# A two-layer hybrid decoder trunk: order and source of prefetched weight operands, and the place of side work

## The chip, the cores and the metric

The kernel runs on one core of one Trainium2 chip. The metric is device time in microseconds of one execution of the whole program; lower is better. The five engines appear below by the short names of the profile: PE (TensorE matmuls; PEld is its weight load), DVE (VectorE), ACT (ScalarE), POOL (GpSimd) and SP (SyncE, which here only issues DMAs).

## The reference

The input is one sequence of 1024 tokens of width 1024. Two layers follow one another. Each has a token mixer, a residual with layer norm, a squared-ReLU MLP of width 4096, a gated embedding and a second layer norm. The mixer of layer 0 is a causal pooling mixer, that of layer 1 a gated DeltaNet.

```python
for i in range(DEPTH):                       # DEPTH = 2
    mix = pool_mixer(...) if i % 2 == 0 else gated_deltanet(...)
    x = layer_norm(DEEPNORM_ALPHA * x + mix, ...)
    ff = square(relu(x @ mlp_w1[i])) @ mlp_w2[i]
    pe = sigmoid(x @ ple_gate_w[i] + ple_gate_b[i]) * (p[i] @ ple_proj[i])
    x = layer_norm(DEEPNORM_ALPHA * x + ff + pe, ...)

# gated_deltanet: 8 heads of 128, chunks of 64 tokens
proj = x @ w_in                              # Q, K, V, z (8 heads each) and two gate logits
q, k, v = silu(causal_conv(proj[Q, K, V], width=4)); q, k = l2norm(q), l2norm(k)
g = cumsum(-exp(a_log) * softplus(a_logit + dt_bias)); decay = exp(g_i - g_j), causal
m = eye + strict_lower(k_beta @ k.T * decay); u, w = triangular_solve(m, [v*beta, k_beta*exp(g)])
for chunk: v_new = u - w @ state
           o = (q*exp(g)) @ state + (q @ k.T * decay) @ v_new
           state = state * exp(g_last) + k_dec.T @ v_new
out = (rmsnorm(o) * norm_w * silu(z)) @ w_out
```

## The kernel before, in words

**Arithmetic.** Matrix products are made from float32 operands that are split in two parts: `split(hi, lo, src)` (L68, L69) copies on ACT to a rounded `hi` and subtracts on DVE to get `lo`. `mm3` (L73 to L75) then makes three matmuls of 128x512. The MLP, the gate's second half and most projections use a seven-product (Strassen-like) scheme over 2x2 blocks, whose products are named P1 to P7.

**Order of the instructions.** The text gives each step a place, and a scheduler then orders every engine's instructions with its own estimates of durations: a step that is ready while an engine is idle may stand some units ahead of its place in the text. Each engine and each DMA queue then runs strictly in that order, and waits where an operand or a free buffer is late. The buffers that matter are rotating slots: `tmp` (six of 128x512), `raw` (three of 128x1024), `wsm` with tags `wh` and `wl` (two each of 128x1024), `big` (ten of 128x4096) and eight PSUM banks.

**Stages, in order of time.** Layer 0's mixer and gate (0 to about 170 us); its MLP, `mlp(0, ...)`, with a phase A of 112 steps (`order`, up to about 487 us) and a phase B of 56 steps (`seq`, up to about 797 us); the projections of layer 1, `project(...)`, first in 18 units (`units`: the gate logits, K heads 0 to 7 and z heads 0 and 1, two halves of the sequence each), then in pairs of heads, `by_pairs` (957 to 1192 us); the chunk recurrence, `chain(...)` (`prepare` and `run`, eight chunks of 128 tokens, up to about 1345 us); the mixer's output product `mix_out` in two halves of the columns (to about 1440 us); layer 1's gate and `mlp(1, ...)` (1497 us to the end).

**Side work in the MLP of layer 0.** `mlp(0, ..., side=parts)` takes one of 101 closures at every second step of phase A (L544, while n is under 110) and, in phase B, two at each of the steps 24 to 39 and one at each step from 40 (L556). The first 13 closures (`k_parts`, L625) read the weights of K heads 2 to 7, split them and store both parts in DRAM (`wk_d`); the other 88 (`pair_parts`, L586) make the seven left operands of each of the 11 pairs and store them in `ws_d`.

**The units.** `weights(u + 1)` fetches the next head's operands before unit u's matmuls: `load_k` (L642) reads the two stored parts straight into `wh` and `wl`, `load_wsm` (L77) reads raw weights into a `raw` slot and splits them. After each unit's matmuls the side list of that unit runs: `gates` at unit 3 (DVE, ending in `g`, L842), `sums` at unit 5 (PE, L851), and pairs of `decay_rhs` (two POOL selects each, L862) at the units 5, 6, 8, 10, 11, 13, 15, 16, each followed one unit later by `decay` (two PE matmuls, an ACT exponential, a POOL select L874, a store to `dt_d`). `couple` makes the strictly lower matrices from them at the units 12 to 19 and stores them in `ad_d`, and `lanes_load` reads all of them back into `L` (2 MB, L926).

**The pairs.** In `by_pairs` the 77 products of 11 pairs run in the list `order`. `prep(n)` (L1000) loads the operand of product n from `ws_d` into one of seven slots, five products ahead. `head` runs the convolution on DVE (three instructions of 128x1023 to 128x1021, L1017) for Q and V heads, and two ACT instructions for z heads; `done` applies Silu and stores to `kqv_d`; `norm_q` transposes Q heads on PE (L1031). A forward substitution on `L` (`substitute(m)`, L942 and L944, m from 62 down to 1) is spread over the products up to number 67 by a running budget, from product 6 on. `load0` starts the loads of chunk 0 near the end.

**The chain.** `load_kqv(n)` loads K, Q and V of a chunk from POOL's DMA queue; `load(n)` loads the triangular blocks (`X`, `a_d`), `t11` from `t_d`, the gates `szt` on SP, and the decays `dt` (L1249, 512 KB into a `raw` slot) and `kt` on POOL's queue. `kq`, `kv`, `merge_a`, `merge_b`, `solve`, `state_in`, `state_out`, `output`, `norm` and `turn` are the steps of a chunk; `turn` scales the output on ACT (L1361), transposes it on PE (L1366) and multiplies by the gates (L1367). `embed1` runs beside it, with small loads `praw` on SP (L226). After the last chunk `fill` holds the products of `mix_out(..., nh=0)`; `mix_left` splits their left operand into `wsm` slots for even t and `raw` slots for odd t.

Of the kernel before, what the change touches and what calls it, by code (L numbers as in the profile page):

```python
# [7 lines left out]
F32 = mybir.dt.float32  # L8
# [24 lines left out]
def trunk(ctx: ExitStack, tc: tile.TileContext, io: dict):  # L33
# [286 lines left out]
    def mlp(i, r1, cut_t3, acc, row, finish=None, ahead=None, out=None, side=()):  # L320
# [21 lines left out]
        with tc.tile_pool(name=f"mlp{i}", bufs=5) as q:  # L342
# [192 lines left out]
            for n, o in enumerate(order):  # L535
                if n + 3 < len(order):
                    prep_a(*order[n + 3])
                if n == len(order) - 2:

                    for c in range(4):  # L540
                        load_w2(c)
                    prep_b(*seq[0])
                multiply_a(*o)
                if side and 2 <= n < 110 and n % 2 == 0:  # L544
                    side.pop(0)()
            for n, (k, g) in enumerate(seq):
# [9 lines left out]
                for _ in range(2 if 24 <= n < 40 else n >= 40):  # L556
                    if side:
                        side.pop(0)()
# [24 lines left out]
    pairs = [("Q", 0), ("V", 0), ("z", 2), ("Q", 2), ("V", 2), ("z", 4), ("Q", 4), ("V", 4), ("Q", 6), ("V", 6), ("z", 6)]  # L583
# [39 lines left out]
    wk_d = [dram.tile([P, 2, 2, 512], F32, name=f"wk{h}_d", tag=f"wk{h}_d") for h in range(2, 8)]  # L623

    def k_parts(h, z):  # L625

        t = {}

        def load():
            t["w"] = new_tmp(F32, "w")  # L630
            nc.sync.dma_start(t["w"], io["w_in"][jof["K"] + h][:, 4 * z:4 * z + 4, :].rearrange("p k c -> p (k c)"))

        def cut():
            hi, lo = new_tmp(F32R, "hi"), new_tmp(F32R, "lo")
            split(hi, lo, t.pop("w"))
            for a, r in enumerate((hi, lo)):
                nc.sync.dma_start(wk_d[h - 2][:, a, z], r.bitcast(F32))

        return load, cut

    def load_k(h):
        w = [wsm.tile([P, 8, P], F32R, tag=t, name=nm(t)) for t in ("wh", "wl")]  # L642
        for a, t in enumerate(w):
            nc.sync.dma_start(t.bitcast(F32).rearrange("p k c -> p (k c)"), wk_d[h - 2][:, a].rearrange("p z c -> p (z c)"))
        return w

    def staggered(pairs):

        pairs = list(pairs)
        return [pairs[0][0]] + [lambda a=a, b=b: (a[1](), b[0]()) for a, b in zip(pairs, pairs[1:])] + [pairs[-1][1]]  # L650

    parts = staggered(k_parts(h, z) for h in range(2, 8) for z in range(2))
    parts += [f for p in range(len(pairs)) for f in pair_parts(p)]
# [140 lines left out]
    def project(gd, pool, x2, left, first, g, ex, ahead, load0):  # L794
# [191 lines left out]
        def by_pairs(pool, ts, b):  # L986
# [13 lines left out]
            def prep(n):  # L1000
                p, k = order[n]
                tag, pl_ = slots[n % 7]
                o = pl_.tile([P, 2, 4, P], F32R, tag=tag, name=nm("wp"))
                nc.sync.dma_start(o.bitcast(F32).rearrange("p z k c -> p (z k c)"), ws_d[p][k].rearrange("p z c -> p (z c)"))
                st.setdefault(p, dict(op={}, ps={}))["op"][k] = o
# [72 lines left out]
            for n, (p, k) in enumerate(order[:last]):  # L1078
                room += 2.72 - (0.4 if pairs[p][0] == "z" else 1.45)
                while n > 5 and m > 0 and (room > 0 or n == last - 1):  # L1080
                    steps.setdefault(n, []).append(m)
                    room -= 0.4 + 2.1e-3 * m * (63 - m)
                    m -= 1
# [35 lines left out]
        at(5, sums)  # L1119
        todo = [(gi, n) for gi in range(2) for n in range(8)]  # L1120
        for k, (gi, n) in enumerate(todo):
            u = (5, 6, 8, 10, 11, 13, 15, 16)[k // 2]
# [56 lines left out]
        def weights(k):  # L1179
            if k < len(units):  # L1180
                s, h, hf = units[k]
                key = (s, h)
                if key not in w:
                    w[key] = load_k(h) if s == "K" else load_wsm(io["w_in"][jof[s] + h])
# [30 lines left out]
    def chain(gd, g, ex):  # L1215
# [19 lines left out]
        def load(n):  # L1235
# [13 lines left out]
            G.dma_start(dt, dt_d[n].rearrange("g p c -> p g c"))  # L1249
# [106 lines left out]
        def turn(n, gi):  # L1356
            d = pre[n]
            o = d["c"][:, 6 + gi]
            for j in range(4):
                c = 16 + gi * 4 + j  # L1360
                A.activation(o[:, j], o[:, j], AF.Copy, scale=d["f"][:, c:c + 1])  # L1361
            if gi == 0 and n % 4 == 0:
# [22 lines left out]
        def run(pool, stats):  # L1385
# [52 lines left out]
            for k, f in enumerate(fill):  # L1438
                if k == 3:
                    both(turn, 7)  # L1440
# [15 lines left out]
    def mix_left(oT, t, nh):  # L1456

        if nh == 0 and t % 2:
# [28 lines left out]
    with tc.tile_pool(name="l1", bufs=4) as pool:  # L1487
# [4 lines left out]
        for t in range(8):  # L1492
            mix_out(oT, wk, acc, stats, t, 1)
# [70 lines left out]
```

## Time and profile before

| | us |
|---|---|
| median of three runs | 2173.79 |
| lowest and highest of them | 2167.78, 2174.63 |
| the profiled execution | 2162.4 |
| its span, first to last instruction | 2160.5 |
| PE busy in the span | 2096.6 (97%) |
| DVE busy | 1588.8 (74%) |
| ACT busy | 1088.8 (50%) |
| POOL busy | 70.8 (3%) |
| mean granted TensorE clock | 0.991 |

Busy times of the engines overlap. A matmul counts as busy until its modelled end, so a busy PE may still run at a lower pace. The granted clock is a share of full speed: 1.00 is 2.4 GHz and 0.50 is 1.2 GHz; a mean between them over a stretch tells how much of it ran at the lower level.

### The profile page before, as it was taken

The numbers are of one execution on the slowest core, as the hardware profiler recorded it, in microseconds if no ns is written. First come the engines' busy times: TensorE is split into PE (matmuls) and PEld (weight loads), VectorE is DVE, ScalarE is ACT, GpSimd is POOL, SyncE is SP. The second block draws the span as 40 slices with busy tenths as digits, with TensorE's granted clock in tenths as the row PEclk, the third lists the DMA queues.
The fourth block names the chain that finished last, engine by engine and source line by source line (L and its number), as shares of the span: only waits on it lengthen the run. The fifth ranks groups of instructions, "written<-read, shape, count | busy, mean of one in ns | idle before, by whom it ended". The sixth has DMA issues, their size and how long they took to land.

```text
span 2160.5 us, 28250 instructions
## 1 busy us (share of the span) xinstructions
PE 2096.6 (97%) x10110; PEld 1745.9 (81%) x10110; DVE 1588.8 (74%) x2647; ACT 1088.8 (50%) x1861; POOL 70.8 (3%) x116
## 2 busy tenths in 40 slices
PE   8999999999999999999999889999999999999998
PEld 7888888877877887877887878778788888888887
DVE  7996787768975977779995468488666666785476
ACT  6425666653544656743445556353355555433343
POOL 0000000000000003310000110000000000000000
PEclk9999999999999999999999999999999999999999
DMA  8326877779785743677779975312344445953242
GB/s 310 108 88 219 286 272 260 258 271 331 265 271 173 258 138 124 188 228 238 233 239 305 286 220 189 101 60 81 119 151 155 152 143 175 327 176 116 97 137 88
DMA packets 233554, 423.19 MB, mean 196 GB/s; under 512 B 45635, under 2 KB 92099, under 8 KB 232133
## 3 DMA queue, kind: packets, MB, share of 16 engines
q1 hardware_dynamic: 224340, 392.55, 54.9%
q0 software_dynamic: 4464, 20.45, 2.7%
q10 hardware_dynamic: 4608, 8.39, 1.0%
q8 instruction: 79, 1.29, 0.3%
q14 instruction: 63, 0.51, 0.1%
HBM read 267.71 MB, written 153.62 MB: 195 GB/s over the span
## 4 chain that ended last, share of the span: by engine, by line
PE 77%; DVE 9%; DMA 7%; ACT 3%; issue 2%; SPq 1%; POOL 0%; DVEq 0%; ACTq 0%; POOLq 0%
PE ps L73 23%; PE ps L75 23%; PE ps L74 23%; DVE u L942 2%; DVE L L944 1%; DMA praw<-in_pT 1%; DMA a<-in_w_in 1%; DVE xy L1017 1%; DMA raw<-in_w 1%; PE ps L1314 1%; PE ps L143 1%; PE ps L1302 1%; PE ps L1336 1%; PE ps L1307 1%; PE ps L910 1%
## 5 line engine op out<-in xcount | busy, mean ns | idle before, releaser
L74 PE MATMUL ps<-rl,lh 128*128 128x512 f32 x896 | 348.8, 389 | 0.2 <-DVE rl L490 0.2
L73 PE MATMUL ps<-rh,lh 128*128 128x512 f32 x880 | 343.2, 390 | 1.5 <-DVE acc L505 1.2
L75 PE MATMUL ps<-rh,ll 128*128 128x512 f32 x880 | 342.8, 390 | 0.8 <-DVE ll L69 0.8
L68 ACT CAST lh<-raw 128x1024 fp32r<-128x1024 f32 x112 | 118.0, 1054 | 251.3 <-PE ps L74 238.8
L69 DVE TENSOR_TENSOR rl<-w,rh 128x1024 fp32r<-128x1024 f32 x108 | 131.8, 1222 | 116.1 <-issue 69.3
L73 PE MATMUL ps<-xh,wo 128*128 128x512 f32 x512 | 199.6, 390 | 1.4 <-ACT c L411 1.4
L75 PE MATMUL ps<-xh,wo 128*128 128x512 f32 x512 | 199.2, 389 | 0.0
L74 PE MATMUL ps<-xl,wo 128*128 128x512 f32 x512 | 199.2, 389 | 0.0
L74 PEld LDWEIGHTS ps<-rl,lh 128*128 128x128 f32 x896 | 168.2, 188 | 35.7 <-DVE rl L490 0.5
L73 PEld LDWEIGHTS ps<-rh,lh 128*128 128x128 f32 x880 | 165.2, 188 | 36.8 <-DVE acc L505 2.1
L75 PEld LDWEIGHTS ps<-rh,ll 128*128 128x128 f32 x880 | 165.2, 188 | 36.6 <-DVE ll L69 2.3
L68 ACT CAST wo<-raw 128x512 fp32r<-128x512 f32 x192 | 118.6, 619 | 103.3 <-DVE raw L340 49.3
L69 DVE TENSOR_TENSOR wo<-raw,wo 128x512 fp32r<-128x512 f32 x192 | 131.2, 687 | 30.5 <-ACT wo L68 30.1
L73 PE MATMUL ps<-xt,wo 128*128 128x512 f32 x384 | 150.0, 391 | 2.9 <-ACT c L402 1.9
L75 PE MATMUL ps<-xt,wo 128*128 128x512 f32 x384 | 149.6, 389 | 0.0
L74 PE MATMUL ps<-xt,wo 128*128 128x512 f32 x384 | 149.5, 389 | 0.0
L69 DVE TENSOR_TENSOR ll<-raw,lh 128x1024 fp32r<-128x1024 f32 x112 | 136.5, 1219 | 3.8 <-ACT lh L68 3.7
L341 DVE TENSOR_TENSOR c<-ps,c 128x512 f32<-128x512 f32 x96 | 66.1, 689 | 76.6 <-ACT c L411 41.2
L68 ACT CAST rh<-w 128x1024 fp32r<-128x1024 f32 x108 | 112.9, 1047 | 6.4 <-DMA h_d<-c 2.8
L73 PEld LDWEIGHTS ps<-xh,wo 128*128 128x128 f32 x512 | 96.1, 188 | 22.4 <-ACT c L411 2.2
L75 PEld LDWEIGHTS ps<-xh,wo 128*128 128x128 f32 x512 | 96.1, 188 | 20.0
L74 PEld LDWEIGHTS ps<-xl,wo 128*128 128x128 f32 x512 | 96.1, 188 | 20.0
(354 smaller groups left out, 4562.3 us busy)
## 6 DMA issues: line engine op xcount, KB each, us to landing
raw<-h_d SPq DMA_DIRECT2D x112, 512.0 KB, 3.8
wp<-ws_d SPq DMA_DIRECT2D x77, 512.0 KB, 4.6
raw<-in_w SPq DMA_DIRECT2D x64, 512.0 KB, 4.7
w<-in_w SPq DMA_DIRECT2D x32, 1024.0 KB, 7.5
h_d<-c SPq DMA_DIRECT2D x64, 512.0 KB, 3.0
ws_d<-hi SPq DMA_DIRECT2D x77, 256.0 KB, 3.5
ws_d<-lo SPq DMA_DIRECT2D x77, 256.0 KB, 3.6
h_d<-hs SPq DMA_DIRECT2D x32, 512.0 KB, 3.7
```

What stands on the lines that cost most here:

```text
L68: A.copy(hi, src)
L69: V.tensor_tensor(lo, src, hi.bitcast(F32), ALU.subtract)
L73: T.matmul(ps, lh, rh, start=first, stop=False, skip_group_check=more)
L74: T.matmul(ps, lh, rl, start=False, stop=False, skip_group_check=more)
L75: T.matmul(ps, ll, rh, start=False, stop=last, skip_group_check=more)
L143: T.transpose(pss[q][:, j, :], y[:, k * P:(k + 1) * P], ident)
L341: add = lambda o, a, b: V.tensor_tensor(o, a, b, ALU.add)
L910: T.matmul(ps[:, j, :], kc, kc, start=True, stop=True)
L942: V.tensor_tensor(v, L[:, a:b, m:m + 1].broadcast_to(shape), L[:, m:m + 1, m + 1:64].broadcast_to(shape), ALU.mult)
L944: V.tensor_tensor(L[:, a:b, m + 1:64], L[:, a:b, m + 1:64], v, ALU.add)
L1017: V.scalar_tensor_tensor(y[:, d:S], x[:, 0:S - d], cw[:, j, c:c + 1], y[:, d:S], ALU.mult, ALU.add)
L1302: T.matmul(pk[:, j, :], hc("K", n, h), St[:, h, :], start=True, stop=True)
```

## The change

The change has these edits.

1. The `k_parts`, `wk_d`, `load_k` and `staggered` helpers are deleted. K heads 2 to 7 are fetched by `load_wsm` in the units, as z heads were: one raw load, one ACT copy and one DVE subtraction of 128x1024 per head.
2. The pairs run in another order: z4 moves from sixth to tenth place, so that the last two pairs are z4 and z6, and the pairs Q4, V4, Q6, V6 come one place earlier.
3. The operands of the last pair (z6) are no longer made in the MLP. `from_weights` reads four raw tiles into `tmp` slots inside `by_pairs`, makes four additions and splits each of the seven operands when it is prepared. The side list shrinks from 101 to 80 closures.
4. In the MLP of layer 0 phase A takes closures while n is under 100 instead of 110, and phase B takes one at each step from 24 on, never two.
5. The substitution starts at product 10 instead of 6.
6. `sums` moves from unit 5 to unit 6; the `decay_rhs` pairs move from units 5, 6, 8, 10, 11, 13, 15, 16 to 7, 8, 9, 10, 11, 13, 15, 16.
7. The load of `dt` in the chain moves from POOL's DMA queue to SP's.
8. `turn` is cut in `scale` and `transpose`; for chunk 7 `scale` runs before the second of the six remaining output products and `transpose` before the third, instead of both before the fourth.
9. `mix_left` puts the operands of t from 4 on (nh = 0) in two `big` tiles; for nh = 1 it is called for t and t + 1 ahead of product t.

```diff
-                if side and 2 <= n < 110 and n % 2 == 0:
+                if side and 2 <= n < 100 and n % 2 == 0:
                     side.pop(0)()
...
-                for _ in range(2 if 24 <= n < 40 else n >= 40):
-                    if side:
-                        side.pop(0)()
+                if side and n >= 24:
+                    side.pop(0)()
...
-    pairs = [("Q", 0), ("V", 0), ("z", 2), ("Q", 2), ("V", 2), ("z", 4), ("Q", 4), ("V", 4), ("Q", 6), ("V", 6), ("z", 6)]
+    pairs = [("Q", 0), ("V", 0), ("z", 2), ("Q", 2), ("V", 2), ("Q", 4), ("V", 4), ("Q", 6), ("V", 6), ("z", 4), ("z", 6)]
...
-    parts = staggered(k_parts(h, z) for h in range(2, 8) for z in range(2))
-    parts += [f for p in range(len(pairs)) for f in pair_parts(p)]
+    parts = [f for p in range(len(pairs) - 1) for f in pair_parts(p)]
...
+            def from_weights(p, k, o):
+                j = jof[pairs[p][0]] + pairs[p][1]
+                if k == P1:
+                    for z in range(2):
+                        for f in range(2):
+                            raw[f, z] = new_tmp(F32, "w")
+                            nc.sync.dma_start(raw[f, z], io["w_in"][j + f][:, 4 * z:4 * z + 4, :].rearrange("p k c -> p (k c)"))
+                a1, a2, b1, b2 = raw[0, 0], raw[0, 1], raw[1, 0], raw[1, 1]
+                if k == P6:
+                    raw["s3"] = new_tmp(F32, "s3")
+                    pl(raw["s3"], a1, b1)
+                    pl(b1, b1, b2)
+                    pl(a1, a1, b1)
+                elif k == P3:
+                    pl(a2, a2, a1)
+                r = {P1: a1, P2: a2, P6: a1, P5: b1, P7: raw.get("s3"), P4: b2, P3: a2}[k]
+                split(o[:, 0], o[:, 1], h4(r))
...
-                while n > 5 and m > 0 and (room > 0 or n == last - 1):
+                while n > 9 and m > 0 and (room > 0 or n == last - 1):
...
-        at(5, sums)
+        at(6, sums)
...
-            u = (5, 6, 8, 10, 11, 13, 15, 16)[k // 2]
+            u = (7, 8, 9, 10, 11, 13, 15, 16)[k // 2]
...
-                    w[key] = load_k(h) if s == "K" else load_wsm(io["w_in"][jof[s] + h])
+                    w[key] = load_wsm(io["w_in"][jof[s] + h])
...
-            G.dma_start(dt, dt_d[n].rearrange("g p c -> p g c"))
+            nc.sync.dma_start(dt, dt_d[n].rearrange("g p c -> p g c"))
...
-                if k == 3:
-                    both(turn, 7)
+                if k == 1:
+                    both(scale, 7)
+                elif k == 2:
+                    both(transpose, 7)
...
-        if nh == 0 and t % 2:
+        if nh == 0 and t > 3:
+            if t % 2 == 0:
+                ready["pool"] = new_big(F32R, "o").rearrange("p (t z k c) -> p t z k c", t=2, z=2, k=8)
+            oh, ol = (ready["pool"][:, t % 2, z] for z in range(2))
+        elif nh == 0 and t % 2:
...
+            for tt in (t, t + 1):
+                if tt < 8 and (tt, 1) not in ready:
+                    mix_left(oT, tt, 1)
             mix_out(oT, wk, acc, stats, t, 1)
```

## Rows read from the trace of the kernel before

**Rows 1.** Page, part 1: busy time, share of span and instructions of each engine

```profile
PE 2096.6 (97%) x10110; PEld 1745.9 (81%) x10110; DVE 1588.8 (74%) x2647; ACT 1088.8 (50%) x1861; POOL 70.8 (3%) x116
```

**Rows 2.** Stretches: length, then each engine's busy time, granted clock, DMA share, GB/s

```profile
470.00:490.00 20.00, 16.59 (x71) 12.53 (x69) 11.82 (x17) 8.79 (x13) 0.00 (x0) 1.00 0.99 321
617.00:705.00 88.00, 85.88 (x375) 69.64 (x374) 54.93 (x68) 37.40 (x44) 0.00 (x0) 1.00 0.63 206
705.00:790.00 85.00, 85.00 (x392) 70.42 (x391) 68.24 (x101) 47.43 (x65) 0.00 (x0) 1.00 0.62 206
832.00:858.00 26.00, 22.77 (x92) 17.73 (x91) 18.25 (x29) 19.21 (x28) 12.79 (x17) 0.87 0.51 158
957.00:1000.00 43.00, 37.34 (x162) 29.97 (x162) 32.40 (x79) 12.19 (x33) 0.00 (x0) 0.96 0.77 272
1174.00:1209.00 35.00, 24.23 (x135) 20.59 (x134) 9.49 (x16) 15.99 (x31) 7.69 (x14) 0.80 1.03 344
1249.00:1267.00 18.00, 10.39 (x73) 9.58 (x71) 6.71 (x21) 5.79 (x26) 2.32 (x4) 0.72 0.65 226
1838.00:1858.00 20.00, 19.32 (x86) 15.68 (x85) 14.50 (x19) 10.10 (x14) 0.00 (x0) 1.00 0.95 338
```

**Rows 3.** Waits of PE, whole span: releaser, us in total, times, longest

```profile
PE ps L1302 <- DVE ctr L1338: 7.6, 1, 7.6
PE ps L1290 <- DMA kqv<-kqv_d: 5.1, 1, 5.1
PE ps L73 <- ACT xy L1060: 4.4, 1, 4.4
PE ps L73 <- DVE L L944: 4.1, 1, 4.1
...
PE ps L75 <- DVE ol L69: 2.9, 1, 2.9
PE ps L1031 <- ACT xy L1021: 2.4, 5, 1.2
...
PE ps L851 <- DVE g L842: 1.8, 1, 1.8
...
PE ps L870 <- POOL dh L862: 1.1, 1, 1.1
```

**Rows 4.** Timeline of POOL, two stretches: start, us, instruction

```profile
851.11 1.61 POOL L862 TENSOR_SCALAR_AFFINE_SELECT dh<-gh 128x512 fp32r<-128x512 f32 x1
...
877.75 0.63 POOL L862 TENSOR_SCALAR_AFFINE_SELECT dl<-gl 128x512 fp32r<-128x512 f32 x1
```

**Rows 5.** Timeline of SP's DMA queue from 957 us: start, us to issue

```profile
959.30 0.32 SPq L926 DMA_DIRECT2D L<-ad_d  x1
...
960.19 1.01 SPq L1004 DMA_DIRECT2D wp<-ws_d  x2
```

**Rows 6.** Chain of waits in order of time: start, us, what (three pieces)

```profile
959.30 8.74 DMA L<-ad_d
...
1192.73 11.01 DMA t<-t_d
...
1239.63 20.44 DMA praw<-in_pT x2
```

**Rows 7.** Timeline of POOL, 1188 to 1196 us: the V load of chunk 0

```profile
1192.70 0.54 POOL L1230 DMA_DIRECT2D kqv<-kqv_d  x1 [12.36 <-DMA X<-xd_d]
```

**Rows 8.** DMA queues, 1238 to 1258 us: packets, MB, share of 16 engines

```profile
q0 software_dynamic: 1239, 5.57, 74.2%
q1 hardware_dynamic: 2625, 0.78, 16.4%
```

**Rows 9.** Waits of POOL, 1160 to 1345 us

```profile
POOL raw L1249 <- PE ps L1366: 17.6, 3, 6.5
POOL raw L1249 <- DVE pll L69: 15.1, 1, 15.1
```

**Rows 10.** Page, part 5: costs of one split, by size (busy, mean ns of one | idle before)

```profile
L69 DVE TENSOR_TENSOR rl<-w,rh 128x1024 fp32r<-128x1024 f32 x108 | 131.8, 1222 | 116.1 <-issue 69.3
...
L69 DVE TENSOR_TENSOR wo<-raw,wo 128x512 fp32r<-128x512 f32 x192 | 131.2, 687 | 30.5 <-ACT wo L68 30.1
...
L68 ACT CAST rh<-w 128x1024 fp32r<-128x1024 f32 x108 | 112.9, 1047 | 6.4 <-DMA h_d<-c 2.8
```

## What I predict, before the changed kernel is built

> **What bounds the kernel now.** The page's first part comes first. PE is busy for 2096.6 of 2160.5 us [rows 1], and no edit removes a matmul. So only what PE loses can be won: about 64 us of idle time, part of it at the start and end, and what it loses at the lower clock. The stretches [rows 2] and PE's waits [rows 3] show where the edits touch that. In a stretch the idle time is its length less PE's busy time. A mean clock c below 1.00 means that a share 2(1-c) ran at 1.2 instead of 2.4 GHz; half of that time, times PE's busy share, is lost as well. I call the sum of the two the loss. The row 705 to 790 has none and shows what this MLP does when fed.
>
> | stretch [rows 2] | idle | clock loss | loss |
> |---|---|---|---|
> | 470-490, MLP phases A to B | 3.4 | 0 | 3.4 |
> | 617-705, two closures per step | 2.1 | 0 | 2.1 |
> | 832-858, gates and decays | 3.2 | 3.0 | 6.2 |
> | 957-1000, start of the pairs | 5.7 | 1.5 | 7.2 |
> | 1174-1209, end of the pairs, chunk 0 | 10.8 | 4.8 | 15.6 |
> | 1249-1267, chain | 7.6 | 2.9 | 10.5 |
>
> With the wait of 2.9 us for `ol` [rows 3] that is 48 us in reach, not all of it meant by an edit.
>
> **MLP of layer 0: -4.8 us.** The same phase change in layer 1, which has no side work, idles 0.7 us in 20 us, against 3.4 in layer 0 [rows 2]. After the edit the last closure stands at n = 98, some 30 us ahead of the change, so I expect layer 1's figure: -2.7. From step 24 of phase B there will be one closure per step. That is what 705-790 already has, with no idle time, so the 2.1 us of 617-705 go. The closures of phase A become pair parts from the start (two splits and additions where a `k_part` had one split), but 21 fewer are made in all. ACT and DVE hide them; if they did not, I would expect single waits like those above. Bounds: -6 to 0.
>
> **Gates and decays: -2.5 us.** PE waits 1.8 us for `g` at `sums`, then 1.1 us for a POOL select [rows 3], and the clock falls behind that. `sums` one unit later (24 matmuls, at 85.00/392 us each 5.2 us) covers the first wait. The second may grow: the decays now fill the units 7 to 11 without a gap. A unit then has four selects for the next one and two for its own, and a select took 0.63 or 1.61 us [rows 4]. At the short one a unit needs 3.8 us and fits; at the long one 9.7 us, 4.5 more than a unit, for some four units 18 us. I take the first wait and a little of the clock. Bounds: -6.2 to +18; the far end is a rival below.
>
> The slow select of the two lies beside DVE work on `right_a`, whose operands are in SBUF [rows 4]. The Trainium skill, "SBUF — State Buffer", section "Who interferes with whom", says that a DVE instruction with two SBUF inputs contends with a GpSimd instruction that reads SBUF. The new K splits put six more such subtractions into these units. By that rule the long price would hold for more selects than before, which speaks against this edit.
>
> **Later substitution: -1.5 us.** The 4.1 us wait that is put down to `L944` [rows 3] is not the substitution's. The operand `wp` of product 3 was issued at 960.19, right behind the 2 MB load of `L` at 959.30 [rows 5], which took 8.74 us [rows 6]; I read the wait as one for that `wp`. The edit moves neither issue, so I leave that loss in place. What it does free is DVE's queue: the steps of products 6 to 9 stand ahead of the first Q heads' convolutions, for whose Silu PE waits five times, 2.4 us together, at most 1.2 [rows 3]. The first two go. The steps no longer taken early go into product 10 and the last one; DVE was idle enough at the end (9.5 of 35 us busy in 1174-1209 [rows 2]). Bounds: -7.2, if the order of SP's queue changes too, to +2.
>
> **Pair order and last pair, end of the projection: -8 us.** PE waits 5.1 us for chunk 0's V [rows 3]. POOL issued that load at 1192.70, after a wait of 12.36 us [rows 7], because the pair V6 is last but one and its stores come at the end. Two pairs of z behind V6 bring them one pair earlier (7 products of 12 matmuls, some 18 us), so this wait goes, and with it part of the 4.8 us clock loss. The 4.4 us wait on `ACT xy L1060` [rows 3] is ACT standing on chunk 0's work in front of a copy of the pairs; nothing removes that. The next late datum is chunk 1's `t`, which landed at 1203.7 [rows 6], 4 us after V. So I take 5.1 plus 2.9 of clock, not all 15.6. `from_weights` adds seven splits and four additions of 128x512, 11 x 0.69 = 7.6 us on DVE [rows 10], beside the two z pairs, which have no convolution. It also holds five of the six `tmp` slots just before the eight `lt` copies to `t_d` need them, which can make `t` late. Bounds: -15.6 to +4.
>
> **`dt` on SP's queue: -4 us.** The 7.6 us wait in the chain [rows 3] is DVE standing on a small split for `embed1`, whose `praw` load took 20.4 us with its neighbour [rows 6]. In that stretch POOL's queue q0 held 74.2% of the DMA engines and SP's q1 16.4% [rows 8], since three chunks' loads left POOL together, after it had waited for a `raw` slot for `dt` (17.6 us in three waits and 15.1 in one in the chain, [rows 9]). Without `dt`, POOL issues K, Q, V and `kt` earlier and more evenly. Against it, SP's queue now holds the `raw` waits, and X, `t`, `szt` and `praw` stand behind them. I take under half of the 10.5. Bounds: -10.5 to +23.
>
> The Trainium skill, "Trainium Kernel Development and Optimization", section "Key Constraints", says that DMAs of SP, ACT and POOL share the same 16 engines and that issuing from several only saves issue time. By that rule moving `dt` wins no bandwidth: the 5.57 and 0.78 MB of the two queues in those 20 us [rows 8] keep their sum, and the -4 would be 0. The trace agrees on the sharing, but its 16.4% for q1 shows that the queue decides who is late.
>
> **End of chain and output product: -3 us.** The `ol` wait of 2.9 us [rows 3] is a split that stands on chunk 7's transpose and on a slot. With the transpose one product (5.2 us) earlier and tiles of their own for t = 4 to 7 it is covered. The call ahead for nh = 1 saves some tenths. Bounds: -4 to +1 (the two `big` tiles come late).
>
> **K weights split in the units: +2 us.** Six heads cost 1.22 us DVE and 1.05 us ACT each [rows 10], in two units of 5.2 us; DVE is busy 18.3 and ACT 19.2 of 26 us there [rows 2]. It fits, but both queues run in order, and the ACT copy can stand for a slot. Against it, three 512 KB transfers per head fall to one. Bounds: 0 to +7.
>
> **Sum.** -4.8 - 2.5 - 1.5 - 8 - 4 - 3 + 2 = -21.8. The profiled execution took 2162.4 us and becomes 2140.6, or 0.9899 of it. It was faster than all three runs shown (2167.78 to 2174.63). Of the median 2173.79 the same share gives **2152 us**, -1.0%. A difference under 0.3% (6.5 us) can't be told from none, so faster ends at 2167 and slower begins at 2180.
>
> **Rivals.**
> - *The waits are passed on.* At the end of the pairs `t` takes V's place, in the chain nothing is won: -21.8 + 8 + 4 = -9.8, 2164 us. For it speaks `t` at 1203.7; against it that V's earlier load also empties q0 sooner. Chance 0.20, a third of it within 0.3%. For the chain's half of it stands the rule of the Trainium skill ("Trainium Kernel Development and Optimization", "Key Constraints") that was named above.
> - *POOL becomes the bound of the decays.* Long selects in units 7 to 11: -21.8 + 2.5 + 18, 2172 us. For it speaks the 1.1 us wait, which came with only two such units in a row; against it the select at 877 us, which took 0.63 beside convolutions [rows 4]. Chance 0.10. The port rule of the Trainium skill ("SBUF — State Buffer", "Who interferes with whom") is the page's way to this one.
> - *SP stands on `dt` (slower).* The `raw` waits of 32.7 us [rows 9] move to SP. It decides where one exceeds the lead of the loads behind it, and chunk 1's `t` had a lead near zero [rows 6]. If 5 us of each of four are covered, 13 us reach PE, and with a clock loss of equal size, as in 1249-1267 for half the stretch, 23: -21.8 + 4 + 23 and, as chunks 0 and 1 lose their gain of 8 too, +13, 2187 us. Chance 0.12.
> - *It does more.* With the losses at `L`, `L1060` and in the chain all gone: -40, 2134 us. Chance 0.10.
> - *The substitution's edit does nothing*, since the scheduler may already order by readiness: +1.5, inside the range.
>
> **How the numbers follow.** Forecast 0.48, the rivals 0.20, 0.10, 0.12, 0.10. Faster: 0.48 + 0.13 + 0.10 = 0.71; within: 0.07 + 0.10 = 0.17; slower: 0.12. The range leaves out the slower rival and the far half of the better one, and so runs from 2134 to 2174 us.
>
> **What would show it.** Right: no PE wait over 1 us in 470-490 and 617-705; no PE wait on `g`; `PE L1290` no longer waiting for `kqv`; no wait of 7 us at `L1302`; none on `ol`. Still there: 4 us near the first products of the pairs, put down to `L944` or a `wp`. Wrong: PE waits on POOL `dh` or `dl` over 3 us in sum; `SPq L1249` standing over 5 us with PE waiting on X, `t` or `szt`; PE waiting on `wh` or `wl` in the K units; `lt` late behind `tmp`.

## The result and the profile after

The changed kernel took 2149.03 us (median of four runs, 2144.98 to 2151.18), beside 2170.78 us for the kernel before: a ratio of 0.9897, 95% interval 0.9871 to 0.9923. The forecast was 2152 us. In a second comparison the changed kernel again took 2149.09 us, but the kernel before 2164.06: 0.9944, interval 0.9924 to 0.9963. So the change is worth 15 to 22 us, and what moves between the comparisons is the kernel before.

Page, part 1, of the changed kernel [rows 1]. With the same 10110 matmuls PE is busy 6.9 us less and idle 10.4 us less, in a span shorter by 17.3 (2143.3 us).

```profile
PE 2089.8 (98%) x10110; PEld 1746.0 (81%) x10110; DVE 1594.2 (74%) x2641; ACT 1089.1 (51%) x1853; POOL 68.2 (3%) x108
```

The stretches of [rows 2] at the same places of the program, with the columns of that group (the two undisturbed ones are left out, and 849 to 875 us is added):

```profile
469.00:489.00 20.00, 19.32 (x85) 15.68 (x85) 15.59 (x20) 10.48 (x15) 0.00 (x0) 1.00 0.98 339
616.00:704.00 88.00, 88.00 (x390) 72.90 (x389) 46.67 (x58) 36.52 (x39) 0.00 (x0) 1.00 0.35 114
823.00:849.00 26.00, 26.00 (x127) 21.68 (x126) 18.71 (x34) 20.24 (x29) 6.15 (x14) 1.00 0.35 100
849.00:875.00 26.00, 23.02 (x94) 17.26 (x93) 25.86 (x23) 23.51 (x34) 22.63 (x23) 0.93 0.47 155
948.00:991.00 43.00, 36.42 (x156) 29.64 (x155) 32.79 (x79) 10.46 (x28) 0.00 (x0) 0.92 0.76 266
1168.00:1203.00 35.00, 27.54 (x164) 23.84 (x163) 5.78 (x17) 18.49 (x38) 5.76 (x11) 0.85 1.05 352
1241.00:1259.00 18.00, 11.83 (x96) 10.64 (x95) 7.45 (x26) 7.29 (x31) 1.59 (x3) 0.81 0.86 280
```

The MLP's two stretches idle 0.7 and 0 us instead of 3.4 and 2.1, and the gates none instead of 3.2. But the stretch behind the gates, which had no idle time before (858 to 884 us there), now idles 3.0 us at a clock of 0.93, with DVE busy 25.9 of 26 us: that loss moved on by one stretch. The start of the pairs got worse: 6.6 us idle and a clock of 0.92, against 5.7 and 0.96. The last two still lose. PE's waits, as in [rows 3]:

```profile
PE ps L73 <- DMA wp<-ws_d: 6.6, 1, 6.6
PE ps L1299 <- DVE oT L1366: 6.2, 1, 6.2
PE ps L1023 <- ACT xy L1013: 3.5, 5, 1.4
...
PE ps L73 <- ACT phl L68: 2.5, 1, 2.5
...
PE ps L1256 <- DMA t<-t_d: 2.0, 1, 2.0
PE ps L839 <- POOL dh L831: 1.4, 2, 0.9
```

Gone are the waits on `kqv` (5.1), `ol` (2.9) and `g` (1.8). The 4.1 us put down to `L` is now 6.6 and carries its true name, `wp`. The 7.6 us of the chain became 6.2.

**By stage.** Each profile was cut at PE's first product with `wo`, with `wb`, with `wp`, after the last with `wp`, and at the first with `wo` of layer 1 (in the changed kernel 173.0, 788.7, 948.8, 1186.3 and 1523.6 us). Medians and stages in us; "chain" includes the output product and gate of layer 1, whose part, from PE's first product with `wkh` on, stands in the last column. "Changed, again" is the changed kernel, timed and profiled a second time.

| kernel | median | MLP of layer 0 | units | pairs | chain | of it output and gate |
|---|---|---|---|---|---|---|
| before | 2170.8, 2164.1 | 624.8 | 160.3 | 234.3 | 348.9 | 205.3 |
| changed | 2149.0 | 615.7 | 160.1 | 237.5 | 337.3 | 199.2 |
| changed, again | 2149.1 | 615.3 | 160.0 | 237.9 | 343.4 | 199.7 |
| old rate | 2151.6 | 616.5 | 160.0 | 238.5 | 344.0 | 201.3 |
| K parts stored | 2162.9 | 622.6 | 161.4 | 234.0 | 348.4 | 201.9 |
| old gates | 2150.9 | 615.5 | 163.5 | 237.0 | 337.9 | 199.3 |
| early substitution | 2148.8 | 615.3 | 160.1 | 238.8 | 341.4 | 201.1 |
| old order | 2163.1 | 615.3 | 160.1 | 238.6 | 355.3 | 201.1 |
| all pairs stored | 2163.4 | 615.4 | 160.0 | 235.2 | 355.9 | 201.0 |
| old order, all stored | 2163.9 | 615.7 | 160.1 | 236.9 | 354.5 | 201.2 |
| dt on POOL | 2153.1 | 615.6 | 160.1 | 236.9 | 350.8 | 200.0 |
| old output | 2155.9 | 615.3 | 160.0 | 239.3 | 349.8 | 207.2 |
| L later, praw early | 2149.6 | 615.5 | 160.1 | 231.5 | 349.3 | 197.0 |
| L on POOL, praw early | 2160.6 | 615.4 | 160.1 | 248.5 | 336.1 | 197.5 |

The MLP and the units repeat to 0.4 and 0.1 us where their code is equal. The chain doesn't: the changed kernel's own two profiles are 6.1 us apart, nearly all of it ahead of the output product, so a difference there is read from the medians. Some profiled executions also lie at the edge of their kernel's runs: those of dt on POOL (2159.1 us) and old output (2158.6) are the slowest of six, that of L on POOL (2153.7) is the fastest of twelve.

The pairs and the chunks together, up to the output product, take 377.9 us before and 375.6 and 381.6 in the changed kernel's two profiles. The MLP's 9 us and the 6 of the output product and gate alone make up the 15 us of the second comparison.

### The profile page after: what moved, and what is told of

Read it like the earlier page. It is cut to its first block, busy times and chain, and to the rows that moved or that the text cites. A ratio compares the mean times of both kernels' runs of the same rounds, so it can differ in the third digit from the quotient of the medians.

```text
span 2143.3 us, 28078 instructions
## 1 busy us (share of the span) xinstructions
PE 2089.8 (98%) x10110; PEld 1746.0 (81%) x10110; DVE 1594.2 (74%) x2641; ACT 1089.1 (51%) x1853; POOL 68.2 (3%) x108
## 4 chain that ended last, share of the span: by engine, by line
PE 80%; DVE 8%; DMA 6%; ACT 3%; issue 2%; SPq 0%; POOL 0%; DVEq 0%; ACTq 0%; POOLq 0%
PE ps L73 25%; PE ps L75 24%; PE ps L74 24%; DVE xy L1009 2%; DVE L L913 1%; DVE u L911 1%; PE ps L143 1%; DMA t_d<-lt 1%; DMA raw<-in_gate 1%; DMA kqv_d<-xy 1%; DMA raw<-in_w 1%; PE ps L879 1%; DMA praw<-in_pT 1%; DMA raw<-in_ple 1%; PE ps L1306 1%
## 5 line engine op out<-in xcount | busy, mean ns | idle before, releaser
L74 PE MATMUL ps<-xl,wo 128*128 128x512 f32 x512 | 199.2, 389 | 0.0
L75 PE MATMUL ps<-xh,wo 128*128 128x512 f32 x512 | 199.2, 389 | 0.0
```

Source lines behind the costliest of these rows:

```text
L74: T.matmul(ps, lh, rl, start=False, stop=False, skip_group_check=more)
L75: T.matmul(ps, ll, rh, start=False, stop=last, skip_group_check=more)
```

## The experiments

All but the first and the last two undo part of the change; times stand against 2149.1 us. The variants ran in four groups, each beside the kernel before, and the changed kernel ran in only one of them. The kernel before read 2163.1 to 2166.6 us in the four; that the changed kernel would have kept its 2149.1 in all is assumed. By the ratio to the kernel before instead, `dt` on POOL would cost nothing (0.9943 against 0.9944), the old output 1 us, the old order 10 and all pairs stored 8.

**The changed kernel again.** Nothing is edited.

> The changed kernel itself, unaltered, as the common yardstick beside the runs of the other variants: the time of the first comparison was 2149 against 2171 us, but the kernel before then ran at 2163 to 2167 us in two later comparisons. If the changed kernel is what the earlier figure says and only the kernel before scatters: 2149 again, ratio about 0.993. If the ratio of 0.990 is right: 2143 to 2145 where the kernel before takes 2165.

2149.09 us, ratio 0.9944: the first case. The kernel before scatters (2149.5 to 2169.3 in these 21 runs), the changed one much less (2147.0 to 2152.0).

**Old rate of the side work.**

```diff
-                if side and 2 <= n < 100 and n % 2 == 0:
+                if side and 2 <= n < 110 and n % 2 == 0:
-                if side and n >= 24:
-                    side.pop(0)()
+                for _ in range(2 if 24 <= n < 40 else n >= 40):
+                    if side:
+                        side.pop(0)()
```

> The changed kernel with the old rates of the side work in the MLP of layer 0 (to step 110 in the first phase, two per step from 24 to 40 in the second); the number of closures stays at 80. Theory (it is where they stand, by the prediction 2.7 us at the change of phase and 2.1 us from 617 to 705): 2153 to 2154, ratio 0.992. Rival (it is how many there are: 21 fewer, and 10 MB less of traffic): 2149, ratio 0.990; the measured gain of the stage was 9.1 us, 1.9 in the first phase and 7.3 in the second, so if rate and number share it, 2153 is half.

The MLP lost some 1 us, at the change of phase; the total, 2151.64 us, is 2.5 more. Of the stage's 9 us the rate is the small part: there the rival holds.

**K weights split in the MLP and stored again**, at the old rate.

```diff
+    parts = staggered(k_parts(h, z) for h in range(2, 8) for z in range(2))
+    parts += [f for p in range(len(pairs) - 1) for f in pair_parts(p)]
...
-                    w[key] = load_wsm(io["w_in"][jof[s] + h])
+                    w[key] = load_k(h) if s == "K" and h > 1 else load_wsm(io["w_in"][jof[s] + h])
```

> The changed kernel with the K weights of six heads split in the MLP of layer 0 and stored again (13 more closures, the old rates), loaded ready-made in the projection's units. Theory (the prediction's terms of -4.8 and +2 us): the MLP of layer 0 loses what the old rate costs and more, 5 to 9 us, and the units gain 2 us, so 2152 to 2156, ratio 0.992. Rival (splitting in the units costs nothing): the units keep their 160 us and the total is 2154 to 2158, ratio 0.993. The difference to the kernel with the old rates alone is the price of the 13 closures themselves.

The thirteen closures cost the MLP 6.1 us over the old rate alone. The longest of PE's waits in this kernel's MLP (172 to 800 us):

```profile
PE ps L73 <- ACT c L407: 3.6, 4, 1.5
```

Four times, early in the first phase, PE stands on an ACT copy `c` out of PSUM; with pair parts in the same places it doesn't. Not all of the 6.1 us is what the kernel before pays: its first phase, with the same thirteen closures, took 309.1 us, here it took 311.7, and with the old rate alone 306.8. The units became 1.4 us longer although they load what they split in the changed kernel. The total is 13.8 us more, beyond theory and rival. The pairs are some 4 us shorter and the chain longer by more than that; why isn't settled.

**Old gates and decays.**

```diff
-        at(6, sums)
+        at(5, sums)
-            u = (7, 8, 9, 10, 11, 13, 15, 16)[k // 2]
+            u = (5, 6, 8, 10, 11, 13, 15, 16)[k // 2]
```

> The changed kernel with sums and decays in their old units (5, and 5, 6, 8, 10, ...). Theory (the prediction's term of -2.5 us): the wait of 1.8 us on g comes back and the POOL select wait of 1.1 us too, so 2151.5, ratio 0.991. Rival (waits only changed place: 2.8 us on dh, dl and xin in the changed kernel stand against 3.2 us on g and dh before): 2149, ratio 0.990, with the wait on g back and the ones on dh, dl near 850 to 868 us gone.

PE's waits from 800 to 890 us:

```profile
PE ps L820 <- DVE g L811: 2.8, 1, 2.8
PE ps L840 <- POOL dl L831: 2.4, 1, 2.4
```

The units are 3.4 us longer, so the edit works as forecast; the median of 2150.85 is only 1.8 us more, which six runs from 2146.9 to 2155.1 can't tell from none. With K stored and loaded the new places cost 1.1 us (161.4 against 160.3 before), with K split they gain 3.4: the two edits belong together.

**Substitution early again** (`while n > 5` for `while n > 9`).

> The changed kernel with the substitution beginning at product 6 again instead of product 10. Theory (the prediction's term of -1.5 us): two of the five waits on the Silu ahead of norm_q come back early in the pairs, 2150.5, ratio 0.991; the wait of 6.6 us on wp stays as it is, since that one is the operand load queued behind the load of L. Rival (the later start has moved the work to where DVE is fuller: five waits of 3.5 us in sum against five of 2.4 before, and a stage 3.2 us longer): faster, 2146, ratio 0.9885, with the stage of the pairs back at 234 us less the wp wait's growth.

2148.82 us: no effect. The waits ahead of `norm_q` are 3.5 us in 5, as without it.

**Old order of the pairs**, the last still from the weights.

```diff
-    pairs = [... ("V", 2), ("Q", 4), ("V", 4), ("Q", 6), ("V", 6), ("z", 4), ("z", 6)]
+    pairs = [... ("V", 2), ("z", 4), ("Q", 4), ("V", 4), ("Q", 6), ("V", 6), ("z", 6)]
```

> The changed kernel with the old order of the pairs (z4 sixth, Q6 and V6 last but two and one, z6 last and still from the weights). Theory (the prediction's term of -8 us, of which the order has the V wait of 5.1 us and some clock): the wait of PE on kqv at chunk 0 comes back with about 5 us and the time is about 2155, ratio 0.993. Rival (V came earlier because fewer bytes stand in the queues at the end, not because of the order): no wait on kqv over 1 us, 2149, ratio 0.990. A second rival for the stage of the pairs, which became 3.2 us longer: if two z pairs at the end, with the last pair's splits, make that, the stage gets back 3 us here and the total is 2149 to 2152.

2163.09 us, 14 more, though the wait on `kqv` is only 3.8. PE's waits:

```profile
PE ps L1256 <- DMA t<-t_d: 7.4, 1, 7.4
...
PE ps L1282 <- DMA kqv<-kqv_d: 3.8, 1, 3.8
```

Waits of 7.3 us on `phl` and 5.4 on a copy of the pairs stand beside them; the forecast had neither these nor the one on `t`.

**All pairs stored**, eight more closures in the MLP.

```diff
-    parts = [f for p in range(len(pairs) - 1) for f in pair_parts(p)]
+    parts = [f for p in range(len(pairs)) for f in pair_parts(p)]
-                if p == len(pairs) - 1:
-                    from_weights(p, k, o)
-                    return
-                if side and n >= 24:
+                if side and n >= 17:
```

> The changed kernel with the last pair stored in DRAM like the other ten: eight more closures in the MLP of layer 0 (its second phase starts with them at step 17 instead of 24), no splits from the weights at the end. Theory (splits at the end are hidden beside z pairs, 7.6 us of DVE there cost nothing): the end of the pairs keeps its time, the MLP loses 0 to 2 us, 2149 to 2151, ratio 0.990 to 0.991. Rival (splitting at the end costs the 3.2 us by which the stage of the pairs grew): 2146, ratio 0.988, and the stage from the first to the last pair product falls from 237.5 to about 234 us.

2163.38 us, 14 more, where nothing was expected. The pairs are 2 us shorter, as the rival had it, but chunk 1 waits for `t`:

```profile
PE ps L1253 <- DMA t<-t_d: 14.4, 2, 13.1
```

SP's DMA queue from 1140 to 1210 us (packets, MB, share of 16 engines), first of this kernel, then of the changed one, then of the one with the old order:

```profile
q1 hardware_dynamic: 13532, 15.06, 68.5%
```

```profile
q1 hardware_dynamic: 13327, 12.42, 59.1%
```

```profile
q1 hardware_dynamic: 13630, 8.80, 46.5%
```

SP's queue moves 2.6 MB more, which is the difference between seven loads of 512 KB and four of 256 KB, and at the 352 GB/s of 1168 to 1203 us it takes 7.5 us. But these bytes don't explain the late `t`: with the old order SP's queue moved 3.6 MB less than in the changed kernel, and PE waited 7.4 us for `t`. What the late kernels share is the order in SP's queue, here from 1184 to 1195 us (this kernel first, then the changed one):

```profile
1189.19 5.37 SPq L1000 DMA_DIRECT2D sz_d<-xy  x1
1194.61 0.57 SPq L1236 DMA_DIRECT2D t<-t_d  x1
```

```profile
1184.19 0.63 SPq L1239 DMA_DIRECT2D t<-t_d  x1
1186.72 0.66 SPq L1003 DMA_DIRECT2D sz_d<-xy  x1
```

Here chunk 1's `t` left behind the store of the last z head, for which SP waited on ACT (5.7 us), and 10.4 us later than in the changed kernel, where it went ahead of the last two z stores. It stands behind the last z store with the old order too (1190.9), with both (1192.4) and in the kernel before (1192.7), and ahead of both in every other variant here but `L later`, at 1181.2 to 1185.9. From its issue it took 7.9 us to land. No run changes this order alone, so how much of the 14 us it makes isn't separated from the bytes.

**Both of these.**

> The changed kernel with the old order of the pairs and the last pair stored again, both together (each alone cost 14 us). Theory A (each edit removes its own wait): the losses add, 2177, ratio 1.005. Theory B (both feed the same shortage: DMA traffic at the end of the projection is full, and the chain's first loads come after it): no more than one of them alone by much, 2163 to 2168, ratio 0.999 to 1.001, with the waits on t and kqv of chunks 0 and 1 in one place. In both the last pair's seven loads of 512 KB stand again where four of 256 KB stood.

2163.88 us: theory B. `t` 9.9 and `kqv` 2.6 us stand where 7.4 and 3.8 stood:

```profile
PE ps L1253 <- DMA t<-t_d: 9.9, 1, 9.9
...
PE ps L1279 <- DMA kqv<-kqv_d: 2.6, 1, 2.6
```

Neither edit wins anything without the other, and in all three kernels chunk 1's `t` stands behind the last z store. SP's queue moves 12.37 MB from 1140 to 1210 us, as much as in the changed kernel. The total is that of the kernel before (ratio 1.0008, interval 0.9993 to 1.0022), though the MLP is 9 us and the output part 4 us shorter, so the pairs and chunks are some 13 us longer than before.

**dt on POOL's queue again** (`G.dma_start(dt, ...)`).

> The changed kernel with one edit undone: the dt load is issued by POOL again. Theory (the prediction's term of -4 us): it gives the 4 us back, so about 2153 against 2149 for the changed kernel, ratio 0.992, and PE waits in the chain grow from one of 6.2 us to something like the 7.6 us of before plus its clock. Rival 1 (the engines are shared, so the queue does not matter): 2149, ratio 0.990, the wait of 6.2 us behind praw stands unchanged. Rival 2 (SP standing on dt is what still costs the 6.2 us): faster, about 2141 to 2145, ratio 0.987, with that wait gone because praw is no longer queued behind a standing dt.

2153.12 us, 4.0 more, as the theory had it (nothing by the ratio, as said above). The profile is that of the slowest of the six runs (2159.1 us). DMA queues from 1238 to 1258 us [rows 8], first of this kernel, then of the changed one:

```profile
q0 software_dynamic: 1148, 5.60, 75.9%
q1 hardware_dynamic: 2492, 0.73, 16.0%
```

```profile
q0 software_dynamic: 841, 4.01, 52.5%
q1 hardware_dynamic: 2912, 1.57, 31.2%
```

The shares are those of before, and so is the wait in the chain (7.7 us). The longest wait is another, which no theory had: with `dt` on POOL's queue PE waits for `t` as well.

```profile
PE ps L1256 <- DMA t<-t_d: 9.3, 3, 5.2
PE ps L1294 <- DVE ctr L1330: 7.7, 1, 7.7
```

**Old output product.**

```diff
-                if k == 1:
-                    both(scale, 7)
-                elif k == 2:
-                    both(transpose, 7)
+                if k == 3:
+                    both(turn, 7)
...
-        if nh == 0 and t > 3:
-            if t % 2 == 0:
-                ready["pool"] = new_big(F32R, "o")...
-            oh, ol = (ready["pool"][:, t % 2, z] for z in range(2))
-        elif nh == 0 and t % 2:
+        if nh == 0 and t % 2:
...
-            for tt in (t, t + 1):
-                if tt < 8 and (tt, 1) not in ready:
-                    mix_left(oT, tt, 1)
```

> The changed kernel with the three edits of the output product undone: shared tiles for t = 4 to 7, scale and transpose of chunk 7 together ahead of the fourth product, no call ahead for the second half. Theory (the prediction's term of -3 us): the wait of 2.9 us on ol comes back, 2152, ratio 0.9915. Rival (the stage from the output product to the MLP became 6.1 us shorter by these edits, half of it in the call ahead for the second half): 2155, ratio 0.993, with further waits in the second half's eight products.

2155.85 us, 6.8 more, the rival's size. Besides the old wait on `ol` one on `wkh` returns:

```profile
PE ps L75 <- DVE ol L69: 2.9, 1, 2.9
...
PE ps L73 <- ACT wkh L68: 2.3, 1, 2.3
```

The output part takes 207.2 us, against 197.0 to 201.9 in all kernels with the new output and 205.3 before: this gain shows in the traces too, whatever the group.

**L later, praw early**: an attempt at the two longest waits left.

```diff
-        at(20, lanes_load)
+                if n == 1:
+                    lanes_load()
-                while n > 9 and m > 0 ...
+                while n > 5 and m > 0 ...
-            nc.sync.dma_start(sz_d[h, :, cols(hf)], sg)
+            A.dma_start(sz_d[h, :, cols(hf)], sg)
...
+            i = nh * 8 + t + 2
+            if i < 16:
+                load_p(i % 8, i // 8)
```

> The changed kernel with two of its remaining waits attacked. (1) The 2 MB load of L is issued behind the first seven wp loads of the pairs instead of behind the second, the z stores of the units leave by ACT's queue, and the substitution may begin at product 6 again. (2) The small praw loads of the embedding in the chain are issued two units ahead instead of one. Theory: the wait of 6.6 us on wp is caused by L in front of it and goes, with some 3 us of clock behind it; the wait of 6.2 us in the chain is DVE standing on a late praw and goes, with some 3 us of clock: 2149 less 12 to 19, 2130 to 2137, ratio 0.985 to 0.988. Rival 1 (the substitution bounds the end, so L later makes xd and t later and the gain at the front is given back there): only the chain's part stays, 2140 to 2143. Rival 2 (the 6.2 us only pass to the next late load, a ctr or an X): 2139 to 2143. Both rivals together: 2149.

2149.6 us, both rivals at once. The wait on `wp` is gone and the pairs are 6.4 us shorter. In the changed kernel that `wp` left right behind the z stores and `L` and took 9.6 us to land; here both are out of its way, so how much each had isn't separated. DVE now ran the last substitution steps behind other work, and the store of `xd` left at 1154.25 us instead of 1138.16. PE's waits, and SP's from 1165 to 1216 us:

```profile
PE ps L1258 <- DMA t<-t_d: 14.6, 2, 10.4
...
PE ps L1301 <- DVE ctr L1332: 6.6, 1, 6.6
```

```profile
SPq L1227 <- DMA sz_d<-xy: 10.0, 1, 10.0
```

`xd` leaves 16 us later and `t` costs 14.6 us, but the first isn't shown to make the second. The longer wait (10.4 us) is for chunk 1's `t`, which left at 1195.11: SP stood 10.0 us in front of it, on the load of chunk 0's gates, whose store hadn't landed. In the changed kernel that load stands behind `t`. In the chain the early `praw` only passed the long wait to `ctr`.

**L on POOL's queue, substitution due earlier.**

```diff
-            nc.sync.dma_start(L, ad_d.rearrange(...))
+            G.dma_start(L, ad_d.rearrange(...))
-            last = len(order) - 9
+            last = len(order) - 16
```

(with `n > 5` and `praw` as above)

> The changed kernel with the load of L issued by POOL instead of SP, so that no wp load stands behind it in a queue; the substitution's steps from product 6 and all due seven products earlier, so that DVE takes them ahead of the last pair's splits as it does in the changed kernel; and praw two units ahead. The run before it in this study removed the wp wait (the pairs became 6.4 us shorter) and lost as much in chunks 0 and 1, where t came 16 us after the place it has in the changed kernel relative to the run's start. Theory (it was the place of the last substitution steps in DVE's order that gave the gain back): the store of xd comes at about 1135 to 1140 us as in the changed kernel, waits on t stay under 5 us in sum, and 6 to 9 us are won, 2140 to 2143 against 2149, ratio 0.990. Rival 1 (DVE is full, so that convolutions now come later and V's or the last pair's copies wait instead): 2149, with new waits on xy or kqv. Rival 2 (L on POOL's queue takes the DMA engines from wp all the same): the wait on wp stays at 4 us or more.

2160.62 us: both rivals' waits, and 11.5 us more than the changed kernel, which neither forecast. No wait on `t` is left (chunk 1's left at 1181.2, ahead of the gates' load), but PE's waits have two others:

```profile
PE ps L73 <- DMA wp<-ws_d: 5.9, 1, 5.9
PE ps L73 <- ACT wp L68: 4.7, 1, 4.7
```

The `wp` load took 9.5 us to land with `L` beside it in another queue as well, and the last pair's splits became late. No version of this study beats the changed kernel.

## Why the prediction was right, point by point

The total was right, and the signs of most terms; how they came together was not, and in that the number was lucky. Pairs, substitution and `dt` were to bring 13.5 us; from the first product of the pairs to the output product the kernel before takes 377.9 us and the changed one 375.6 and 381.6. The MLP and the output product brought 9 and 6 where 4.8 and 3 were forecast.

- *MLP, -4.8.* The sign was right, the size short: 9 us, outside the bounds of -6 to 0. The step that failed is "21 fewer are made in all. ACT and DVE hide them": the closures got no price. The old-rate run gives 1 us to the rate, to which I had given all, and the K-parts run 6.1 to thirteen closures, 4.9 of it in phase A, where I had forecast nothing. It is no clean share (the kernel before loses only some 2 us in phase A), and the eight closures of the last pair cost nothing at the new rate (615.4 us with all pairs stored).
- *Gates -2.5, K split +2.* Right in sum: the units measured -0.2 against -0.5. The 6.2 us of the gates' stretch didn't go, though: much of them moved to 849 to 875 us, where DVE is full (3.0 us idle and a clock of 0.93, a loss of 4.6 us by the prediction's reckoning). Waits on `dh`, `dl` came to 1.9 us in the first profile and to 3.1 in the second, just over the 3 that I had named as a sign of being wrong; POOL still did not become the bound. The old-gates run shows that the +2 would have been +3.2 with the old places, and the K-parts run that it is -1.3 with the new. Two readings were wrong. The select at 877 us did not run "beside convolutions": DVE ran nothing beside it, and beside convolutions a select took 1.08 us (last section). And in the units two transfers of 512 KB per head fell to one, not three. PE's waits on the selects in the second profile (800 to 890 us):

```profile
PE ps L839 <- POOL dh L831: 1.7, 3, 0.9
PE ps L840 <- POOL dl L831: 1.4, 2, 0.9
```

- *Substitution, -1.5.* Nothing; the rival that the edit does nothing holds. My reading of the 4.1 us wait held as far as the runs go: it is `wp` behind `L`, and also behind the z stores that stand ahead of `L`. Where three `wp` loads left ahead of `L` PE waited 4.1 us (before), 4.7 (old gates) and 3.5 (K parts), a wait that the profile names after DVE there; with two ahead of it 6.6 (changed), with seven, and the z stores in another queue, not at all. That the third load slips behind `L` is the cost that I missed. SP's queue in the changed kernel, start and us [rows 5]:

```profile
947.94 2.75 SPq L1098 DMA_DIRECT2D sz_d<-tmp  x2
950.86 0.32 SPq L895 DMA_DIRECT2D L<-ad_d  x1
951.23 0.93 SPq L977 DMA_DIRECT2D wp<-ws_d  x2
```

- *Order and last pair, -8.* The mechanism for V held (no wait on `kqv`), and so did `t` as the next late datum (2.0 us here, more where an edit is undone). Undone singly, either part costs 14 us, and both together 15; done, they show no gain of that size over the kernel before. What I missed is the place of chunk 1's `t` in SP's queue. I looked for its delay in the splits on DVE and in the `tmp` slots, which "can make `t` late"; in the runs it is late where it stands behind the last z store, which is so in every kernel with an edit undone here, and in the kernel before, where PE waited only 1.0 us for it because V and a copy of the pairs had held it up first (5.1 and 4.4 us). Undoing the last pair makes `t` late, not doing it.
- *dt, -4.* The medians give 4.0, the size forecast, with the doubt about the groups named above. But it isn't shown as a gain by itself. Taken singly, the parts come to 9 (MLP stage), 3 (gates), 0, 14 (order or last pair), 4 and 7 us, 37 in sum, where the whole change is worth 15 to 22. With old order and stored pairs the pairs and chunks are some 13 us longer than before, and the edits left there are `dt`, the substitution and what the units pass on. That `dt` on SP's queue makes `t` wait, as the slower rival had it, isn't borne out: with `dt` on POOL's queue PE waits 9.3 us for `t`, and in the kernel before chunk 1's `t` left at the same place. What makes the 13 us stays open. The prediction added terms which depend on each other, and the sum came out because the errors did.
- *Output product, -3.* More: 6.8 by the medians, 6 by the traces. The `ol` wait went as said. A wait on `phl` of 2.5 us took its place, for the same chunk 7 transpose; but one on `wkh` of 2.3 went too, which I hadn't seen.
- *Waits passed on.* Half of this rival came true: in the chain 6.2 us remain of 7.6, again on a split for `embed1`. The chain of waits in order of time, the load first:

```profile
1237.36 13.39 DMA praw<-in_pT
1250.82 0.41 ACT phl L68
1251.26 0.07 DVE phl L69
1251.60 0.70 DVE oT L1366
```

"No wait of 7 us at L1302" was met by its number and not by its sense.

## What to carry to other kernels

Before a load is moved or an operand is made elsewhere, look at what stands in each queue in front of the next datum that PE will wait for, stores that wait for another engine as well as bytes: here `t` was late behind a z store, with 8.80 MB in its queue and with 15.06. A sum of terms assumes that they are independent; parts that feed the same full stretch (1.05 of the DMA engines at 1168 to 1203 us) are to be costed together, and undone together to see it. A wait that is removed early in a stage can come back at its end, as in `L later`, where the pairs became 6.4 us shorter and the next stage's `t` took it back. And a stage in which one kernel's two profiles differ by 6 us can't settle a term of 4.

## What the runs showed of the hardware

**POOL's selects and DVE's operands.** Timeline of POOL in the changed kernel, then of DVE beside it (start, us):

```profile
835.09 0.63 POOL L831 TENSOR_SCALAR_AFFINE_SELECT dh<-gh 128x512 fp32r<-128x512 f32 x1 [0.16 <-issue]
...
850.01 1.61 POOL L831 TENSOR_SCALAR_AFFINE_SELECT dh<-gh 128x512 fp32r<-128x512 f32 x1
851.58 0.63 POOL L831 TENSOR_SCALAR_AFFINE_SELECT dl<-gl 128x512 fp32r<-128x512 f32 x1
...
856.34 1.08 POOL L831 TENSOR_SCALAR_AFFINE_SELECT dl<-gl 128x512 fp32r<-128x512 f32 x1
```

```profile
835.02 0.69 DVE L857 TENSOR_REDUCE kn<-tmp 128x4 f32<-128x512 f32 x1 [0.26 <-ACT tmp L853]
...
849.59 1.53 DVE L1129 TENSOR_TENSOR r<-xh,xh 128x1024 f32<-128x1024 f32 x1
851.05 0.67 DVE L857 TENSOR_REDUCE kn<-tmp 128x4 f32<-128x512 f32 x1
...
855.81 1.12 DVE L946 SCALAR_TENSOR_TENSOR K<-xin,cw,K 128x512 f32<-128x512 f32 x1
```

A select takes 0.63 us beside a reduction of one operand, 1.61 where it starts during a DVE instruction that reads two tensors of 128x1024, and 1.08 where it starts during a convolution step, which reads two of 128x512. The select at 851.58 keeps its 0.63, though the next such DVE instruction starts at 851.65: it was first. The Trainium skill, "SBUF — State Buffer", section "Who interferes with whom", has DVE instructions with two SBUF inputs contend with GpSimd instructions that read SBUF; the trace agrees. The convolution step slows too (1.12 us, against 2.33 for three at 832.44). PE's waits on `dh` and `dl` are 1.9 and 3.1 us in the two profiles; how much of that is the contention isn't isolated.

**Queues.** With `L` on POOL's queue PE still waited 5.9 us for a `wp` on SP's, which took 9.5 us to land (9.6 with `L` on SP's queue). The Trainium skill, "Trainium Kernel Development and Optimization", section "Key Constraints", says that another queue saves only issue time; for this transfer the trace agrees. For `dt` it doesn't settle the matter: the move was worth 4.0 us by the medians and nothing by the ratio, and it changed the order within each queue.
